# A mixer, cross-attention and routed-expert layer: 512 tokens cut as 128 + 384 in place of 256 + 256, with memory's products between the first chunk's

## The chip, the cores and the metric

One core of one Trainium2 chip runs the kernel in one launch. The time is the device time of the launch in microseconds, a median over runs. All operands lie in HBM at the start and the result is written back to HBM. The engines named below are TensorE (PE; its weight loads are PEld in the profile), VectorE (DVE), ScalarE (ACT), GpSimd (POOL), and SP, which here only issues DMAs.

## The reference

One layer over 512 tokens of width 2048, batch 1, in float32, with a memory of 256 rows. What is computed, with the parts that do not matter here left out:

```python
def reference(x, mem, ...):
    h = hybrid_mixer(x, ...)              # products with w_in (2048 x 16 K columns), mLSTM (4 heads),
                                          # forgetting attention (16 heads), both causal over the tokens,
                                          # two branch products, a gate each, w_out
    x = layer_norm(ALPHA * x + h, ...)
    h = memory_cross_attention(x, mem, w_xq, w_xkv, w_xo)    # 4 heads of 512, 256 memory rows
    x = layer_norm(ALPHA * x + h, ...)
    h = peer_ffn(x, peer_wq, sub_keys, expert_u, expert_v)
    return layer_norm(ALPHA * x + h, ...)

def peer_ffn(x, w_pq, sub_keys, expert_u, expert_v):
    q = (x @ w_pq).reshape(B, S, 8, 2, 128)
    sc = einsum('bshpd,hpnd->bshpn', q, sub_keys)            # 8 heads x 2 x 128 keys
    ...  # top 16 of each 128, top 16 of their 256 sums: 128 of 16384 experts a token, weights g
    a = einsum('tkd,td->tk', expert_u[idx], x)
    return einsum('tk,tkd->td', gelu(a) * g, expert_v[idx])
```

Each token uses 8 x 16 = 128 experts, each a row of `expert_u` and a row of `expert_v` of 8 KB. The mixer is causal: a later token needs the keys and values of earlier ones and never the other way round, so the tokens can be processed in chunks.

## The kernel before

**Products.** A weight matrix lies in HBM as groups of 2048 x 512, each four loads of 1 MB (`load_raw`, three buffers `raw`, issued on SP). Each half of a load is split by `split` into a high part and the rest (`whi`, a cast on ScalarE, L137; `wlo`, a subtraction on VectorE, L138), two buffers of each, and a product is three matmuls: high times high, high times low, low times high. `group_ws` keeps the weights stationary and streams the activations' 256 token columns (L165); `group_as` keeps the activations stationary, 128 tokens at a time, and streams 512 weight columns (L206, L207, L214). A group's sums lie in PSUM banks of a pool `mm` with five buffers; an `evac` function takes them out. Small products of the heads and transposes use three other banks (`sm_bank`).

```python
def split(hi, lo, src):
    nc.scalar.copy(hi, src)
    return nc.vector.tensor_sub(lo, src, hi.bitcast(F32))
def load_raw(src):
    raw = wp.tile([P, 2048], F32, tag="raw", bufs=3, name=nm("raw"))
    nc.sync.dma_start(raw, src)
```

**Order.** The 512 tokens are two halves of 256. The program is written in this order:

1. The gates of all 512 tokens from `xT`, which leaves every token's x split in SBUF.
2. First half: `ml_stage` (per head a group for q and k, one for v, one for o; then four pairs of gate and branch groups: 20 groups), `fx_stage` (per four heads q, k, v; then four gate and four branch groups: 20 groups), `residual` with w_out (4 groups), `norm`. Keys, values and convolution tails go to DRAM scratch or stay in `tail`, for the second half.
3. `mem_stage`: for each of 4 heads, memory's keys times w_xq and memory's values times w_xo (64 loads of 1 MB), stored to DRAM as `Ad` and `Bd` by DMAs on POOL's queue. With these, cross-attention is two products: `attend` with `Ad` (2 groups) and a `residual` with `Bd` (2 groups).
4. First half: `attend`, `residual`, `norm`.
5. Second half: the first group of `ml_stage(1)`, then `pick0`: the choice of experts (`choose`: 4 groups of `peer_wq`, `select`, `soften`) for the first half, whose indices go to `ei` and weights to `gg`. From here the gathers can run. Then the rest of the second half's mixer and its end.
6. `choose` for the second half, then the dense weights `gd`: for each token a one-hot of 128 for either key index (L1023, L1025 on VectorE), a matmul, a copy on ScalarE (L1030), a store.
7. Dense experts for the second half: `stage_a` (128 chunks of `uT`, Gelu) runs 32 chunks ahead, `stage_o` multiplies by `gd` and by `vD` and adds into `acc`.

**Gathers.** The first half's 256 tokens do not take the dense way. For each of the two blocks of 128 tokens there are 128 jobs `job_u` and 128 `job_v`. A job is one indirect DMA on POOL (L826) that fetches one row of 8 KB for each of 128 tokens, 1 MB, into one of two buffers `rows`, and one VectorE instruction that uses it: a dot product with the token (`rows`, `x2l`, L851) or an addition into `gacc` (L865).

```python
def job_v(t, k, s):
    rows = gather("peer_v", t, k, s)
    def use(s2):
        ...
        i = nc.vector.scalar_tensor_tensor(acc, rows, d[:, GB + k % GB:GB + k % GB + 1], acc,
                                           op0=ALU.mult, op1=ALU.add)
        after(i, s2)
```

Each weight split calls `tick`. It adds `rate` to a credit; each whole credit emits the next job, whose DMA may not go before that split; its use is emitted `LAG` = 2 ticks later and may not stand before that tick's split in VectorE's order. The rate is 240 jobs in 400 ticks in the second half's mixer and the rest over 490 ticks in the dense stage.

A planner (the framework's list scheduler, with a simulated timeline) then fixes each engine's order: it may take later work first where earlier work is not ready in its simulation. So a gather's use can stand far behind the tick that emitted it. After the last use of a block, `fin_early` normalizes and stores it; `fin` does the same for a dense block.

## Time and profile before

| | us |
|---|---|
| median of 3 runs | 5213.6 |
| range of the runs | 5212.26 to 5215.16 |
| profiled execution | 5213.9 |
| its span, first to last instruction | 5212.2 |
| PE busy in it | 4571.0 |
| VectorE busy | 3851.3 |
| ScalarE busy | 2051.6 |
| POOL busy | 791.8 |
| moved by DMA | 1435.57 MB, mean 275 GB/s |

The span is one execution as the hardware profiler saw it. A matmul's busy time overlaps that of the next, since matmuls are pipelined, so what one costs in a row of them is read from the distance of their starts. "Clock" in a view is the granted TensorE clock as a share of full speed, the DMA share is the mean busy share of 16 DMA engines. The profile's cut into stages used below follows the first and last loads of each matrix.

### The profile page before, as it was taken

How to read it: one execution, taken by the hardware profiler on the slowest of the kernel's cores; microseconds unless marked ns; L12 is line 12 of the kernel's file. 1: busy time of each engine (PE TensorE's matmuls, PEld its weight loads, DVE VectorE, ACT ScalarE, POOL GpSimd, SP SyncE). 2: the span in 40 equal slices, each digit the busy share in tenths (PEclk: the TensorE clock that was granted, in tenths of full speed). 3: DMA queues.
4: the chain of work that ended last, by engine and by line, in shares of the span. 5: the costliest groups of instructions: out<-in, count | busy, mean ns of one | idle time of the engine just before them, and what ended most of it. 6: DMA issues, size and time to landing. Idle time of an engine off the chain costs nothing. (4 is left out here: it accounts for less than half of the span.)

```text
span 5212.2 us, 74619 instructions
## 1 busy us (share of the span) xinstructions
PE 4571.0 (88%) x29998; PEld 4159.8 (80%) x29998; DVE 3851.3 (74%) x5446; ACT 2051.6 (39%) x2665; POOL 791.8 (15%) x676
## 2 busy tenths in 40 slices
PE   9999999999999999998999786967999999999100
PEld 8899999989989878987897586856988889998100
DVE  6654544564458997788878899998788888888655
ACT  5543444454445444444444432323444344444000
POOL 0000000000100022222222222211211112221221
PEclk9999999999999999999999898968999999999555
DMA  5555555666655588988889888977989888898777
GB/s 208 191 188 196 189 187 185 212 212 222 224 206 189 203 320 334 348 321 315 330 338 337 323 329 291 350 238 262 347 335 342 339 333 339 326 342 332 244 252 235
DMA packets 261100, 1435.57 MB, mean 275 GB/s; under 512 B 26668, under 2 KB 68972, under 8 KB 99216
## 3 DMA queue, kind: packets, MB, share of 16 engines
q1 hardware_dynamic: 135360, 831.45, 43.6%
q0 software_dynamic: 85008, 573.23, 30.2%
q10 hardware_dynamic: 40384, 26.12, 1.7%
q8 instruction: 235, 3.85, 0.3%
q14 instruction: 113, 0.93, 0.0%
HBM read 1372.59 MB, written 58.11 MB: 274 GB/s over the span
## 5 line engine op out<-in xcount | busy, mean ns | idle before, releaser
L138 DVE TENSOR_TENSOR wlo<-raw,whi 128x1024 fp32r<-128x1024 f32 x1216 | 1472.7, 1220 | 739.7 <-ACT whi L137 692.3
L137 ACT CAST whi<-raw 128x1024 fp32r<-128x1024 f32 x1216 | 1268.0, 1049 | 1719.5 <-PE mm L165 930.6
L865 DVE SCALAR_TENSOR_TENSOR gacc<-rows,dots,gacc 128x2048 f32<-128x2048 f32 x256 | 600.5, 2346 | 123.8 <-DMA rows<-in_peer_v,ei 122.8
L851 DVE SCALAR_TENSOR_TENSOR rows<-rows,x2l 128x2048 f32<-128x2048 f32 x256 | 584.9, 2285 | 106.2 <-DMA rows<-in_peer_u,ei 106.0
L826 POOL DMA_INDIRECT rows<-in_peer_v,ei x256 | 385.4, 1506 | 1268.9 <-DVE gacc L865 1085.7
L826 POOL DMA_INDIRECT rows<-in_peer_u,ei x256 | 316.5, 1236 | 1601.9 <-DVE rows L851 1065.1
L1054 PE MATMUL pa<-Ch,whi 128*128 128x256 f32 x2048 | 506.3, 284 | 34.7 <-ACT sc L815 25.7
L1055 PE MATMUL pa<-Cl,whi 128*128 128x256 f32 x2048 | 505.7, 284 | 0.0
L1054 PEld LDWEIGHTS pa<-Ch,whi 128*128 128x128 f32 x2048 | 394.3, 193 | 42.2 <-ACT sc L815 25.9
L1108 PE MATMUL mm<-vh,hph 128*128 128x512 f32 x1024 | 400.7, 393 | 19.1 <-ACT hph L137 16.6
L1109 PE MATMUL mm<-vh,hpl 128*128 128x512 f32 x1024 | 400.5, 392 | 5.8 <-DVE hpl L138 5.8
L1055 PEld LDWEIGHTS pa<-Cl,whi 128*128 128x128 f32 x2048 | 394.7, 193 | 5.0
L165 PE MATMUL mm<-Cl,whi 128*128 128x256 f32 x1536 | 379.2, 284 | 4.4 <-DVE Cl L138 4.4
L165 PE MATMUL mm<-Ch,whi 128*128 128x256 f32 x1536 | 381.2, 285 | 0.1
L165 PE MATMUL mm<-Ah,whi 128*128 128x256 f32 x1536 | 379.2, 284 | 0.3 <-ACT whi L137 0.3
L165 PE MATMUL mm<-Bh,whi 128*128 128x256 f32 x1536 | 377.8, 283 | 0.7 <-ACT whi L137 0.7
L165 PE MATMUL mm<-Al,whi 128*128 128x256 f32 x1536 | 377.5, 283 | 0.0
L165 PE MATMUL mm<-Bl,whi 128*128 128x256 f32 x1536 | 377.4, 283 | 0.0
L138 DVE TENSOR_TENSOR vl<-raw,vh 128x1024 fp32r<-128x1024 f32 x256 | 307.2, 1221 | 71.3 <-ACT vh L137 64.0
L137 ACT CAST vh<-raw 128x1024 fp32r<-128x1024 f32 x256 | 265.5, 1050 | 195.2 <-PE mm L1109 165.7
L1059 PE MATMUL pa<-Ch,wlo 128*128 128x256 f32 x2048 | 290.0, 285 | 16.8 <-DVE wlo L138 16.4
L165 PEld LDWEIGHTS mm<-Cl,whi 128*128 128x128 f32 x1536 | 295.5, 193 | 5.6 <-DVE Cl L138 4.9
(338 smaller groups left out, 8992.1 us busy)
## 6 DMA issues: line engine op xcount, KB each, us to landing
raw<-in_w_in SPq DMA_DIRECT2D x256, 1024.0 KB, 4.9
raw<-in_uT SPq DMA_DIRECT2D x128, 1024.0 KB, 6.8
raw<-in_vD SPq DMA_DIRECT2D x128, 1024.0 KB, 6.8
raw<-in_w_br_ml SPq DMA_DIRECT2D x32, 1024.0 KB, 5.2
raw<-in_w_br_fx SPq DMA_DIRECT2D x32, 1024.0 KB, 5.1
raw<-in_w_out SPq DMA_DIRECT2D x32, 1024.0 KB, 5.5
raw<-in_w_xkv SPq DMA_DIRECT2D x32, 1024.0 KB, 5.9
raw<-in_peer_wq SPq DMA_DIRECT2D x32, 1024.0 KB, 5.8
```

Source lines behind the costliest of these rows:

```text
L137: nc.scalar.copy(hi, src)
L138: return nc.vector.tensor_sub(lo, src, hi.bitcast(F32))
L165: i = nc.tensor.matmul(o, w, x, start=start, stop=stop)
L826: i = nc.gpsimd.indirect_dma_start(out=rows, out_offset=None, in_=I[table], in_offset=bass.IndirectOffsetOnAxis(ap=ei[t][:, k:k + 1], axis=0))
L851: i = nc.vector.scalar_tensor_tensor(rows, rows, 1.0, tok[t]["x2l"], op0=ALU.mult, op1=ALU.mult, accum_out=d[:, k % GB:k % GB + 1])
L865: i = nc.vector.scalar_tensor_tensor(acc, rows, d[:, GB + k % GB:GB + k % GB + 1], acc, op0=ALU.mult, op1=ALU.add)
L1054: nc.tensor.matmul(bank[:, :H], uh[:, sl], xh, start=k == 0, stop=False)
L1055: nc.tensor.matmul(bank[:, :H], uh[:, sl], xl, start=False, stop=False)
L1059: nc.tensor.matmul(bank[:, :H], ul[:, sl], X2[k][0], start=False, stop=k == 15)
L1108: nc.tensor.matmul(banks[t][g], a[:, tt], vh[:, gs_], start=c == c0, stop=False)
L1109: nc.tensor.matmul(banks[t][g], b[:, tt], vh[:, gs_], start=False, stop=False)
```

## The change

The tokens are cut into a first block of 128 and a second chunk of 384.

- **First block, mixed with memory.** `ml0` and `fx0` are the mixer for 128 tokens; every group is a `group_as` with one block. All groups are now generators that stop after each 1 MB load. `mix(first_block(), ms, MIX)` takes three steps of the first block's mixer and w_out, then one of `mem_stage`. While this runs there is a second pair of raw buffers (`wx`); alone, `wp` has two, no longer three.
- **First block's end.** `Ends(…, 0, 1, …)` does attention, residual and norm for 128 tokens, then `pick0` chooses for that block, after the chunk's first group as before. The 256 jobs of block 0 are spread over 1040 units; a split counts 3 units in a group over 384 tokens, 2 over 256, 1 over 128.
- **Second chunk.** `ml1` and `fx1` run 384 tokens; `group_ws` streams 384 columns into four banks of one PSUM buffer each, `group_as` does three blocks. The x of these tokens is loaded and split a second time.
- **Split at w_out.** From w_out on the chunk is block 1 (`e1`, 128 tokens, gathered later) and blocks 2 and 3 (`e2`, 256 tokens, dense). Their steps alternate, block 1 ahead; block 1's choice (`pick1`) then stands before the last norm of blocks 2 and 3.
- **Gathers.** Block 1's 256 jobs are added after `pick1`, over 1070 units of the choice and the dense stage (a `uT` split counts 2.1, a `vD` split 2). The lag is 2, then 3 from the dense weights on. The credit is capped at 2.
- **One-hots.** Four tokens at once: two broadcast comparisons of 128 x 512 on VectorE, then four scalings by `g` on ScalarE (in place of 4 + 4 instructions on VectorE, whose second did the scaling).
- **Dense stage.** Two more raw buffers in the pool `main`, used in turn with `wp`'s two. A gathered block's final affine rows are now 1 MB each, in the `rows` buffers, loaded for the gathered block and again for the dense blocks.

The core of the diff:

```diff
-LAG = 2
-EARLY = 240
+MIX = 3
...
+        def mix(a, b, n):
+            live = True
+            for i, _ in enumerate(a):
+                if live and i % n == n - 1:
+                    live = next(b, 0) is None
...
-            raw = wp.tile([P, 2048], F32, tag="raw", bufs=3, name=nm("raw"))
-            nc.sync.dma_start(raw, src)
+            raws["n"] += 1
+            p = raws["pools"][raws["n"] % len(raws["pools"])]
+            raw = p.tile([P, 2048], F32, tag="raw", bufs=2, name=nm("raw"))
+            nc.sync.dma_start(raw[:, :n], src)
...
-        def group_ws(src, X, evac):
+        def group_ws(src, X, nb, evac):
+            n = nb * P
+            per = 2 if nb == 2 else 1
-            banks = [mm_bank() for _ in range(2)]
+            banks = [mm_bank() for _ in range(4 // per)]
...
-            state["credit"] += state["rate"]
+            state["credit"] = min(state["credit"] + state["rate"] * cost, 2.0)
...
-                state["later"].append((n + LAG, f(t, k, s)))
+                state["later"].append((n + state["lag"], f(t, k, s)))
+        def set_rate(units):
+            state["rate"] = (len(jobs) - state["done"]) / units
...
+        raws["pools"].append(wx.enter_context(pool("wx", side="right")))
+        def first_block():
+            with pool("ml0") as mp:
+                yield from ml0(mp, hT, m0)
+            with pool("fx0") as fp:
+                yield from fx0(fp, yT, m0, G0)
+            e["x"] = Ends(e["xs"].enter_context(pool("xa0")), 0, 1, nc.gpsimd, nc.gpsimd)
+            yield from e["x"].residual(G0, I["w_out"], True, 4)
...
+                mix(first_block(), ms, MIX)
+                e["x"].norm(0, X1, pr0, False)
+                drain(ms)
+        wx.close()
...
+        drain(e["x"].attend(X1, pr0, PT))
+        drain(e["x"].residual(PT, Bv, False))
+        e["x"].norm(1, X2, pr0, True)
+        def pick0():
+                c = Choice(pp, pp, 1)
+                drain(c.run(X2, nc.gpsimd))
+                c.indices(0)
+            add_jobs(0)
+            set_rate(1040.0)
+            ticks.append(tick)
+            drain(ml1(mp, X, prB, hT, pick0))
+        drain(fx1(X, prB, yT, prA, G))
...
+        drain(e1.residual(Gb, I["w_out"], True))
+        e1.norm(0, X1b, pr1, False)
+        drain(e2.residual(Gc, I["w_out"], True))
+        drain(e1.attend(X1b, pr1, PTb))
+        e2.norm(0, X1c, lambda: pair(cpl, "X", 16), False)
+        drain(e1.residual(PTb, Bv, False))
+        drain(e2.attend(X1c, pr1, PTc))
+        e1.norm(1, X2b, pr1, True)
+        drain(e2.residual(PTc, Bv, False))
+            drain(c.run(X2b, nc.sync))
+            c.indices(1)
+        add_jobs(1)
+        set_rate(1070.0)
+        e2.norm(1, X2, lambda: pair(fpl, "X", 16), True)
+            drain(c.run(X2, nc.sync))
+        state["lag"] = 3
...
-                        nc.vector.tensor_scalar(o1, iota, selT["i1"][:, c], None, op0=ALU.is_equal)
-                        nc.vector.tensor_scalar(o0, iota, selT["i0"][:, c], selT["g"][:, c],
-                                                op0=ALU.is_equal, op1=ALU.mult)
+                    nc.vector.tensor_tensor(o1, selT["i1"][:, ta:ta + 4].unsqueeze(2).to_broadcast(full), it,
+                                            op=ALU.is_equal)
+                    nc.vector.tensor_tensor(o0, selT["i0"][:, ta:ta + 4].unsqueeze(2).to_broadcast(full), it,
+                                            op=ALU.is_equal)
+                        nc.scalar.activation(o0[:, u], o0[:, u], AF.Copy, scale=selT["g"][:, ta + u:ta + u + 1])
...
+        raws["pools"].append(mn)
-        state["rate"] = (len(jobs) - state["done"]) / 490.0
```

More of the change, by code (lines that the diff above doesn't have):

```diff
@@ L321, in mt, with ml1 @@
+        def ml1(mp, X, hpool, hT, between):
+            n = 384
             def mt(tag, bufs, n=512):
@@ L359, in ev_o @@
                     nc.scalar.activation(ot[t], b, AF.Sigmoid)
[L361 to L362 removed]
+                yield from group_ws(wi[3 * h], X, 3, ev_qk)
+                if h == 0:
                     between()
[L364 to L371 removed]
@@ new lines, in build, with __init__, t, residual @@
+        class Ends:
+            def __init__(self, xp, b0, nb, ld, st):
+                self.xp, self.b0, self.nb, self.ld, self.st = xp, b0, nb, ld, st
+                self.r = [[None] * 4 for _ in range(nb)]
+            def t(self, tag, bufs, n=512):
+                return self.xp.tile([P, n], F32, tag=tag, bufs=bufs, name=nm(tag))
+            def residual(self, X_, W, first, rbufs=12):
+                nb, r = self.nb, self.r
+                self.sts = self.xp.tile([P, 2, 32], F32, tag="sts", bufs=3, name=nm("rst"))
@@ L901, in build, with tick @@
                     jobs.append((job_v, t, k - lag))
-        order = []
-        for i in range(HB):
-            order += [(j, i) for j in jobs if j[1] == i]
-        jobs = [j for j, _ in order]
-        def tick(s):
+        def tick(s, cost):
             n = state["n"] = state["n"] + 1
@@ new lines, in build @@
+        e = {}
+        with pool("memt", side="right") as tp:
+            MT = []
+            for i in range(2):
+                raw = load_raw(I["memT"][i])
+                for q in range(4):
+                    a, b = pair(tp, "M", 16)
+                    split(a, b, raw[:, q * 512:(q + 1) * 512])
+                    MT += parts(a, b, MEM)
+            with pool("mem", side="right") as xp:
+                ms = mem_stage(xp, MT)
+                mix(first_block(), ms, MIX)
+                X1, X2 = [], []
+                e["x"].norm(0, X1, pr0, False)
+                drain(ms)
@@ new lines, in build, with prA @@
+        wx.close()
+        del raws["pools"][1:]
+        big = ExitStack()
+        ap_ = big.enter_context(pool("bigA", side="right"))
+        def prA():
+            return pair(ap_, "A", 32, 384)
+        X = []
+        for i in range(4):
+            raw = load_raw(I["x1T"][i], 1536)
+            for q in range(4):
+                a, b = prA()
+                split(a, b, raw[:, q * 384:(q + 1) * 384])
+                X.append((a, b))
+        PT = []
+        drain(e["x"].attend(X1, pr0, PT))
@@ L1117, in stage_o @@
             if last and dh == 0:
+                if state["done"] < len(jobs):
+                    raise RuntimeError(f"{len(jobs) - state['done']} jobs left")
+            if last and dh:
+                while state["later"]:
+                    state["later"].pop(0)[1](s)
                 fin_load()
```

1074 lines of the change are left out of this document (574 added, 500 removed).

## The prediction

> **What bounds the kernel now.** I read the page's slices first, then the stretches between stage borders, then the DMA issues of four of them, the waits, and the chain at the end.
>
> ```profile
> span 5212.2 us, 74619 instructions
> PE   9999999999999999998999786967999999999100
> PEclk9999999999999999999999898968999999999555
> DMA  5555555666655588988889888977989888898777
> ```
>
> TensorE is full for 37 of 40 slices and then idle: the last three hold no matmul, while DMA goes on. The DMA row has two levels: five or six tenths in the first 15 slices, nine from the 16th on, when the row gathers begin.
>
> ```profile
> 20.00:972.00 952.00, 951.20 (x6772) 891.91 (x6770) 516.11 (x775) 438.54 (x552) 36.64 (x68) 1.00 0.54 190
> 972.00:1067.00 95.00, 95.00 (x484) 81.41 (x483) 53.53 (x55) 38.91 (x39) 3.22 (x6) 1.00 0.62 215
> 1067.00:1447.00 380.00, 368.91 (x2716) 348.67 (x2715) 197.35 (x209) 171.58 (x206) 35.72 (x56) 1.00 0.65 219
> 1447.00:1600.00 153.00, 152.51 (x863) 133.28 (x862) 94.83 (x121) 80.22 (x107) 9.13 (x17) 1.00 0.59 206
> 1600.00:1800.00 200.00, 199.60 (x1302) 180.60 (x1302) 194.45 (x618) 93.66 (x110) 3.09 (x2) 1.00 0.52 181
> 1800.00:2735.00 935.00, 888.23 (x6193) 820.46 (x6192) 755.42 (x898) 396.90 (x497) 207.81 (x142) 0.98 0.88 329
> 2735.00:3035.00 300.00, 254.06 (x1272) 210.69 (x1271) 258.39 (x277) 131.47 (x172) 72.23 (x50) 0.91 0.89 327
> 3035.00:3570.00 535.00, 404.33 (x2780) 365.35 (x2779) 510.69 (x1233) 162.98 (x279) 91.75 (x78) 0.87 0.81 285
> 3570.00:4835.00 1265.00, 1240.64 (x7551) 1113.28 (x7552) 1038.18 (x1075) 520.03 (x675) 249.73 (x159) 0.99 0.89 337
> 4835.00:5212.00 377.00, 8.02 (x35) 5.99 (x33) 221.25 (x174) 6.48 (x12) 77.33 (x81) 0.52 0.72 246
> ```
>
> Columns: stretch, length, then busy us and count of PE, PEld, DVE, ACT, POOL, then clock, DMA share, GB/s. In order: first half's mixer, its w_out, memory's products, first half's cross-attention, its choice of experts with the second half's first group; second half's mixer, its end, second choice with the one-hot build, dense experts, tail. PE bounds the mixers, memory and the dense stage; DVE bounds both choices (194 of 200, 511 of 535); the tail is bounded by gathers.
>
> Gathers issued in 1780 to 2735, 3035 to 3570, 3570 to 4835, 4835 to 5212 (count, size or none, median us to landing), with one weight load beside the first and the uncontended one:
>
> ```profile
> rows<-in_peer_u,ei POOLq DMA_INDIRECT x78, 8.1
> rows<-in_peer_v,ei POOLq DMA_INDIRECT x66, 8.2
> raw<-in_w_in SPq DMA_DIRECT2D x106, 1024.0 KB, 7.0
> ...
> rows<-in_peer_u,ei POOLq DMA_INDIRECT x39, 6.5
> rows<-in_peer_v,ei POOLq DMA_INDIRECT x39, 7.6
> ...
> rows<-in_peer_u,ei POOLq DMA_INDIRECT x80, 7.7
> rows<-in_peer_v,ei POOLq DMA_INDIRECT x79, 8.2
> ...
> rows<-in_peer_v,ei POOLq DMA_INDIRECT x47, 5.5
> rows<-in_peer_u,ei POOLq DMA_INDIRECT x34, 5.5
> ...
> raw<-in_w_xqT SPq DMA_DIRECT2D x16, 1024.0 KB, 4.8
> ```
>
> So 144 of the 512 gathers go out in the second mixer (6.6 us each), 50 in its end (the POOL count above), 78, then 159 beside the dense stage (8.0 us each), and 81 are left when the matmuls end. These cost 377 us: 342 of gathering (4.2 us each) and 35 of finish. The chain of the end is made of such landings, two at a time, each with its use on DVE:
>
> ```profile
> 4863.86 5.46 DMA rows<-in_peer_v,ei
> ```
>
> Waits in the dense stage (total us, times, longest):
>
> ```profile
> POOL rows L826 <- DVE rows L851: 492.9, 64, 14.4
> POOL rows L826 <- DVE gacc L865: 437.1, 70, 13.0
> ...
> DVE gacc L865 <- DMA rows<-in_peer_v,ei: 8.8, 5, 2.8
> ```
>
> POOL waits 930 us for a row buffer; DVE hardly waits for rows. With two row buffers, a landing of 8 us and a place in DVE's fixed order, 8 us a gather is what this stage gives.
>
> **Prices.** Start to start, a 256-column matmul takes 0.12 us, a 512-column one 0.225:
>
> ```profile
> 100.77 0.28 PE L165 MATMUL mm<-Ah,whi 128*128 128x256 f32 x1
> 100.89 0.28 PE L165 MATMUL mm<-Al,whi 128*128 128x256 f32 x1
> ...
> 4822.05 0.39 PE L1108 MATMUL mm<-vh,hph 128*128 128x512 f32 x1
> 4822.28 0.39 PE L1109 MATMUL mm<-vh,hpl 128*128 128x512 f32 x1
> ```
>
> A group (2048x512 weights, four 1 MB loads, 8 splits) is 192 matmuls with weights stationary (23.0 us at 256 columns) or 48 per 128 tokens with tokens stationary (10.8). The first mixer bears it out: 28 groups x 23.0 + 12 x 21.6 = 904, so 48 of its 952 us are heads. For 384 columns no row exists. Bounds: 0.12 and 0.225; I take the middle by length, 0.173, so 33.2 us a group (23 to 43). The Trainium skill, "TensorE: Matmul & The Clock Gate", back-to-back issue gap, has N/2.4 + 2.5 ns: an estimate of 162.5 ns at 384, by which the sum would fall by 27 x 192 x 0.0105 = 54 us; its 216 ns at 512 stands against 225 here.
>
> ```profile
> L138 DVE TENSOR_TENSOR wlo<-raw,whi 128x1024 fp32r<-128x1024 f32 x1216 | 1472.7, 1220 | 739.7 <-ACT whi L137 692.3 <-PE mm L165 27.2 <-PE mm L214 17.5
> L137 ACT CAST whi<-raw 128x1024 fp32r<-128x1024 f32 x1216 | 1268.0, 1049 | 1719.5 <-PE mm L165 930.6 <-PE mm L207 456.8 <-DVE wlo L138 154.6
> L865 DVE SCALAR_TENSOR_TENSOR gacc<-rows,dots,gacc 128x2048 f32<-128x2048 f32 x256 | 600.5, 2346 | 123.8 <-DMA rows<-in_peer_v,ei 122.8 <-ACT stage L1030 0.7
> L1025 DVE TENSOR_SCALAR o<-iota,i0T,gT 128x128 f32<-128x128 f32 x256 | 85.1, 334 | 0.0
> L1023 DVE TENSOR_SCALAR o<-iota,i1T 128x128 f32<-128x128 f32 x256 | 70.3, 276 | 0.2 <-PE mm L1027 0.2
> L770 DVE TENSOR_TENSOR eq<-pf,iota 128x512 f32<-128x512 f32 x32 | 20.3, 675 | 0.0
> L506 ACT COPY pt<-sm 128x128 f32<-128x128 f32 x32 | 8.7, 271 | 0.0
> ```
>
> **The change, part by part.**
>
> *A, first block mixed with memory.* 44 groups of 128 tokens (40 mixer, 4 w_out): 44 x 10.8 = 475. Memory is unchanged, 363 of its 380 us by count (48 loads x 5.76 + 16 x 5.4). Heads about 45 (half of 48 and the added transposes). PE: 883. Against it: 240 MB plus some 22 MB of stores, operands and x; at the 337 GB/s of the dense stage 810 us. DVE: 480 splits x 1.22 = 586, plus half of the first mixer's other work (516 - 390 = 126, so 63) and memory's (41): 690. All fit, none with much room: a 128-token half-load has 1.36 us of PE against a 1.22 us subtraction, on two whi/wlo buffers. I add 40 for that and 20 of start: A ends at 945. Ends: 905 with perfect cover, 1060 if each of the 352 half-loads waited 0.5 us. The block's small loads and memory's 64 stores share POOL's queue: 37 + 36 us of its busy time, with no gather behind them. The other 384 tokens' x is split twice, for the gates here and again in B: 32 splits of 128x384, under 1.22 us each, 39 at most, beside PE's first groups.
>
> *B, first block's end, and its choice.* Attention 2 groups, residual 2, choice 4, chunk two's first group 33. Raw buffers are now two: 0.4 + 4.8 landing + about 3.4 for both splits, over two, is 4.3 us a load against 2.7 of PE, so 32 loads cost 138; with norm 15, the last selection 25 and half of the first group hidden: 205, to 1150 (150 to 270). Gathers begin there, not at 1800.
>
> *C, chunk two, 384 tokens.* 27 x 33.2 + 12 x 32.5 = 1286; heads 1.5 x 53 = 80. Four of five PSUM banks go to a weights-stationary group, so the next one waits for evacuation: some 20 such borders x 1.5 us = 30 (0 if ScalarE empties them in time, 80 if four 0.6 us copies are waited out each time and DVE's are behind a 2.3 us gather step). C: 1396, ends 2546. SP's queue holds kp, vp, nF and m1 behind the raw loads; a raw load now waits for one of two buffers, with 16.6 us of PE per pair against 7.0 + 3.4, so I cost that at nothing; that cover goes if landings pass 9 us. The 256 gathers of block one are due over 1040 units of the 936 here and 224 behind (5.6 us each); at the 6.6 measured they end at 2840, still ahead of the next choice.
>
> *D, ends of blocks two (128) and three to four (256), and block two's choice.* 48 thin loads x 4.4 + 32 x 5.5 = 387, the norms of one beside the products of the other, 30 for the last selection: 418, to 2964. The old end was 300 for 32 loads with its norms bare. Ends: 340 and 530 (7.0 us landings all along).
>
> *E, second choice and build.* DVE decides: selection for two blocks about 130 (194 of the first choice less its 40 splits and a group's convolution), splits 39 + 78 (32 uT chunks ahead), last norm 25, the one-hots 128 x 0.675 = 86 in place of 155, and gathers. The ticks allow only 47 here (choice 64 and chunks 134 units at 256/1070), x 2.35 = 110. Sum 468, at 96% 485. The 256 added scalings on ScalarE, x 0.27 = 69, lie in its idle time (163 of 535 busy); they show only if it is late for a bank. To 3449.
>
> *F, dense stage.* Same matmuls: 1265, to 4714. Lag 3 and four raw buffers I cost at nothing: the gathers run behind their due time, so the lag does not bind, and PE is not waiting for loads (1241 of 1265). Gathers at 8.0 us: 159. Left: 256 - 47 - 159 = 50.
>
> *G, tail.* 50 x 4.1 = 205, finish 40 (35, with the affine rows loaded twice). End: 945 + 205 + 1396 + 418 + 485 + 1265 + 245 = 4959, say 4960. This is a sum of spans; the profiled execution took 1.7 us more than its span (5213.9) and lies 0.3 above the median of three, so nothing is corrected. Differences under 0.2% (10 us) I call the same.
>
> **Rivals.**
>
> *R1, gathers keep up.* For it: only 256 are left after block two's choice, where 318 were left at 3035, and DMA in D is free. Against: 159 in the dense stage was with POOL always holding due jobs. If the stage gave 195 (6.5 us, the second mixer's rate), 14 would be left: 4714 + 57 + 40 = 4811.
>
> *R2, thin loads starve.* Steps of 2.7 us of PE wait for two raw buffers and a busy DVE; A takes 1060, D 530, so the second gathers start 227 later and the end is 5187, a gain of half a percent only. For it: the end stage at 300 us for 173 of PE now. The granted clock falls where PE waits, 0.91 in 2735 to 3035 and 0.52 in the tail; at 0.5 a thin load has 5.4 us of PE in place of 2.7, 1.0 above the 4.4 counted in D, so 48 us more there, within D's upper end. The Trainium skill, "TensorE: Matmul & The Clock Gate", HAM oscillation, says the same of thin products: waits beyond 3.4 us put PE back on half clock at every step; the two clocks agree in kind.
>
> *R3, slower: PSUM banks in C.* If each of the 39 groups stalled PE for evacuation behind DVE's gather steps, at 8 us a group C grows by 312 - 30 = 282 and the end is 5241. It passes the old time at 7.3 us a group. Against: ScalarE, which empties most banks, was 42% busy there (397 of 935), and PE's longest total wait in the old second mixer (1800 to 2735) was for a softmax, 18 us over ten heads:
>
> ```profile
> PE sm L501 <- DVE p L492: 18.2, 10, 3.0
> ```
>
>
> *R4, the tail does not move.* The fixed order defers block two's gathers to the end as before (81 or more left), with stages as forecast: 4714 + 332 + 40 = 5086.
>
> **How the numbers follow.** Forecast 0.47 (4870 to 5040), R1 0.20, R4 0.15, R2 0.09, R3 0.09. A range 4790 to 5180 takes in R1, R4 and most of the forecast's spread, and leaves R3 and the ends of others, about 2 in 10. Faster 0.87 (forecast, R1, R4, most of R2), same 0.03, slower 0.10.
>
> **What would show it.** A: w_out's last load of block one near 930, DMA share about 0.85 there. B: first gather near 1150. C: about 1400 us, 384-column starts 0.17 apart. D: the second 256 gathers start near 2960. E: dense stage starts near 3450 with DVE above 0.95. F: 155 to 165 gathers beside 1265 us. G: 50 gathers behind the last matmul. The prediction is wrong if the first weights of the dense stage come later than 3600, or if the count left at the last matmul is under 20 or over 80.

## The result, and the profile after

The changed kernel takes 5249.5 us (median of 4 runs, 5243.4 to 5252.4) against 5212.9 of the kernel before (4 runs, 5209.8 to 5215.2): a ratio of 1.0069 [1.0052, 1.0086]. It is slower by 0.7 per cent; 4960 had been forecast. The profiled span grew from 5212.2 to 5241.7 us.

The page of the kernel before, its row of TensorE's total, and then the page of the changed kernel: the span, the totals, and three rows of slices.

```profile
PE 4571.0 (88%) x29998; PEld 4159.8 (80%) x29998; DVE 3851.3 (74%) x5446; ACT 2051.6 (39%) x2665; POOL 791.8 (15%) x676
```

```profile
span 5241.7 us, 66469 instructions
PE 4565.4 (87%) x25662; PEld 4021.7 (77%) x25662; DVE 3915.7 (75%) x5122; ACT 2272.1 (43%) x3129; POOL 811.7 (15%) x631
PE   7999999789999999999978887369999999999700
DMA  7888888557777887776878657159998888888767
```

TensorE has the same work as before, 4565 against 4571 us: fewer and wider matmuls, no less time. It is no longer full in the first slice and around the eighth, it has a hole at slices 21 to 27 where the old one had a smaller hole, and it is still idle in the last two. The stretches of the changed kernel, in the order of the prediction's letters A to G (columns as in the prediction: stretch, length, busy us and count of PE, PEld, DVE, ACT, POOL, clock, DMA share, GB/s; POOL's count from C on is gathers). The fourth and fifth rows are cut at 3040, ahead of block two's query weights; the forecast's D runs on to block two's indices, which come at 3177:

```profile
20.00:940.00 920.00, 888.98 (x5040) 758.54 (x5039) 677.99 (x757) 618.83 (x727) 55.00 (x90) 0.99 0.82 303
940.00:1150.00 210.00, 161.83 (x688) 122.27 (x687) 146.94 (x286) 109.63 (x150) 6.44 (x12) 0.92 0.61 216
1150.00:2650.00 1500.00, 1462.29 (x7637) 1327.50 (x7636) 1083.45 (x1419) 514.07 (x695) 334.81 (x228) 0.99 0.75 278
2650.00:3040.00 390.00, 325.22 (x1324) 249.84 (x1323) 295.07 (x341) 185.13 (x240) 47.69 (x28) 0.90 0.74 271
3040.00:3510.00 470.00, 295.78 (x1793) 261.58 (x1791) 371.90 (x1000) 224.24 (x520) 19.04 (x17) 0.83 0.49 167
3510.00:4945.00 1435.00, 1414.99 (x9093) 1288.76 (x9094) 1155.69 (x1166) 606.10 (x775) 278.30 (x177) 1.00 0.88 332
4945.00:5242.00 297.00, 7.68 (x28) 5.83 (x27) 176.29 (x141) 5.86 (x11) 65.28 (x63) 0.52 0.71 247
```

Put against the forecast, with a third column that the first experiment below supplies (the run-ahead put back):

| stage | forecast | changed kernel | with run-ahead |
|---|---|---|---|
| A, to its end | 945 | 940 | 940 |
| B | 205 | 210 | 210 |
| C | 1396 | 1500 | 1500 |
| D, to block two's indices | 418 | 527 | 525 |
| E | 485 | 333 | 470 |
| F | 1265 | 1435 | 1265 |
| G | 245 | 297 | 255 |
| sum | 4959 | 5242 | 5165 |

**Where the time came from, against the kernel before.** As TensorE's work is the same, the end of the matmuls can only move by its idle time. Stretch minus busy, from the rows here, in the prediction and in experiment 1 (the ends and the second choice cut at 3035 and 3040):

| idle TensorE, us | before | changed | with run-ahead |
|---|---|---|---|
| first tokens, memory, first choice | 13 | 79 | 78 |
| the second mixer | 47 | 38 | 37 |
| its ends | 46 | 65 | 66 |
| second choice and build | 131 | 174 | 144 |
| dense stage | 24 | 20 | 14 |
| sum | 261 | 376 | 339 |

So TensorE is idle for 115 us more, and the matmuls end 110 us later (4945 in place of 4835). The tail is 80 shorter (297 in place of 377), because 63 gathers are left in place of 81. 110 - 80 = 30, which is the 29.5 us of the spans. The earlier gathers did bring something; the added idle time took more: 66 us in the first three stages, 19 in the ends and 43 in the second choice and build, of which the blocked queue described next made 30 (elsewhere it is 13 less).

**The hole at slice 26.** SP issues all weight loads through one queue. First the waits of that queue, from 3200 to 3530, with the columns: waiting line, waited for, total us, times, longest:

```profile
SPq L154 <- DMA gd<-stage: 151.8, 3, 128.1
```

then its issues from 3196 on in the changed kernel:

```profile
3196.86 36.92 SPq L154 DMA_DIRECT2D raw<-in_peer_wq  x6
3240.18 156.28 SPq L154 DMA_DIRECT2D raw<-in_uT  x5
3500.37 1.54 SPq L1275 DMA_DIRECT2D G<-gd  x2
```

and in the kernel before:

```profile
3100.76 213.43 SPq L142 DMA_DIRECT2D raw<-in_uT  x25
3317.72 0.33 SPq L835 DMA_DIRECT2D x2l<-x2d  x1
3320.07 37.08 SPq L142 DMA_DIRECT2D raw<-in_uT  x7
```

The old kernel loads 32 chunks of `uT` ahead beside the choice and the build. In the changed one every second load goes to a raw buffer of pool `main`, whose memory still holds the `stage` tiles of the one-hot build; the load waits for their stores, and all loads behind it wait too, in order. DMA stands nearly still:

```profile
3250.00:3380.00 130.00, 38.86 (x217) 35.30 (x216) 119.61 (x428) 35.90 (x110) 3.02 (x3) 0.65 0.12 44
```

Six loads of `uT` go out before 3510, and the run-ahead's products (32 chunks) are done in F instead, which is why F has 1415 us of TensorE in place of 1241.

**The second gathers.** The gathers of the changed kernel around the border of its two blocks (start, us, instruction, idle before it and what ended it):

```profile
2886.59 0.94 POOL L983 DMA_INDIRECT rows<-in_peer_v,ei  x1 [9.86 <-DVE wlo L148]
3177.65 0.94 POOL L983 DMA_INDIRECT rows<-in_peer_u,ei  x1 [290.12 <-DVE ei L969]
```

For 290 us no gather runs: block one is done, and block two's indices `ei` come only at 3177, forecast for 2964.

### The profile page after: what moved, and what is told of

Its sections match the earlier page's. It is cut to its first block, busy times and chain, and to the rows that moved or that the text cites. A ratio compares the mean times of both kernels' runs of the same rounds, so it can differ in the third digit from the quotient of the medians.

```text
span 5241.7 us, 66469 instructions
## 1 busy us (share of the span) xinstructions
PE 4565.4 (87%) x25662; PEld 4021.7 (77%) x25662; DVE 3915.7 (75%) x5122; ACT 2272.1 (43%) x3129; POOL 811.7 (15%) x631
## 5 line engine op out<-in xcount | busy, mean ns | idle before, releaser
L1259 PE MATMUL pa<-Xh,whi 128*128 128x256 f32 x2048 | 503.9, 283 | 32.0 <-ACT whi L147 21.1
L1260 PE MATMUL pa<-Xl,whi 128*128 128x256 f32 x2048 | 503.2, 283 | 0.0
L179 PE MATMUL mm<-Ah,whi 128*128 128x384 f32 x1280 | 439.6, 344 | 8.2 <-DVE qk L612 3.0
L179 PE MATMUL mm<-Al,whi 128*128 128x384 f32 x1280 | 435.6, 341 | 0.0
L1259 PEld LDWEIGHTS pa<-Xh,whi 128*128 128x128 f32 x2048 | 389.9, 190 | 39.4 <-ACT whi L147 21.5
L1260 PEld LDWEIGHTS pa<-Xl,whi 128*128 128x128 f32 x2048 | 388.8, 190 | 6.5
L223 PE MATMUL mm<-whi,Zh 128*128 128x512 f32 x832 | 333.9, 401 | 48.1 <-ACT whi L147 45.9
L224 PE MATMUL mm<-whi,Zl 128*128 128x512 f32 x832 | 331.2, 398 | 1.1 <-DVE Zl L148 1.1
L223 PE MATMUL mm<-whi,Ah 128*128 128x512 f32 x768 | 314.2, 410 | 7.5 <-ACT whi L147 7.5
L224 PE MATMUL mm<-whi,Al 128*128 128x512 f32 x768 | 311.8, 406 | 0.0
```

The lines of the kernel that those rows point to most:

```text
L179: i = nc.tensor.matmul(o, w, x, start=start and s % per == 0, stop=stop and s % per == per - 1)
L223: nc.tensor.matmul(banks[t], xh[:, tt], wh[:, c], start=k == 0, stop=False)
L224: nc.tensor.matmul(banks[t], xl[:, tt], wh[:, c], start=False, stop=False)
L1259: nc.tensor.matmul(bank[:, :H], uh[:, sl], xh, start=k == 0, stop=False)
L1260: nc.tensor.matmul(bank[:, :H], uh[:, sl], xl, start=False, stop=False)
```

## The experiments

All ratios are to the kernel before, in runs on the same chip. The kernel before took 5208.7 to 5217.6 us (medians) beside the different experiments, so a difference of some 10 us between two experiments says little.

**1. The run-ahead put back.** Pool `main` gives its raw buffers only behind the chunks that run ahead.

```diff
         mn = ctx.enter_context(pool("main"))
-        raws["pools"].append(mn)
...
         for a in range(ahead[0]):
             stage_a(a)
+        raws["pools"].append(mn)
```

> Changed kernel with one line moved: the two raw buffers of pool main join only after the 32 uT chunks ahead are written, so that these use the two buffers of wp alone. Theory P (the new raw buffers lie on memory that the one-hot build still uses, so SP's queue stands at them and holds the run-ahead and its gathers): over 30 uT loads and over 40 gathers go out between block two's choice and the start of the dense stage (6 and 17 in the changed kernel), the dense stage takes about 1265 in place of 1435, the last matmul comes near 4800 in place of 4945, 30 to 45 gathers are left (63), the time is 5040 to 5120. Theory G (the gathers decide, two row buffers at 8 us each from block two's choice on, wherever PE is): the loads go ahead too, but what PE gains comes back as more gathers left, 80 to 95, time 5190 to 5250.

5160.8 us (5155.0 to 5166.9), 0.9902 [0.9886, 0.9919]. Its stretches from 3040 on:

```profile
3040.00:3645.00 605.00, 460.89 (x3218) 421.88 (x3216) 507.71 (x1104) 298.73 (x615) 58.31 (x47) 0.92 0.65 230
3645.00:4910.00 1265.00, 1251.02 (x7677) 1125.06 (x7678) 1036.72 (x1073) 532.89 (x681) 222.22 (x155) 0.99 0.89 335
4910.00:5165.00 255.00, 0.84 (x4) 0.38 (x2) 153.47 (x126) 3.76 (x8) 54.56 (x54) 0.51 0.70 254
```

The blocked queue cost 89 us, and without it the change is a gain of 1 per cent. Theory P has the mechanism and not the size: the last matmul comes at 4910, not near 4800, and 54 gathers are left. F is 1265 as forecast, with 155 gathers. The stretch from 3040 to the dense stage, called the choice stretch below, is 605 us with the run-ahead in it; 470 of them lie behind block two's indices (3175), where the forecast's E had 485.

**2. Memory behind the first block, not mixed with it.**

```diff
-                mix(first_block(), ms, MIX)
+                mix(first_block(), ms, 10 ** 6)
```

> Changed kernel, with memory's products after the first block and not between its steps. Theory M (the first block alone would be bound by DMA, 12.4 us a group at 340 GB/s against 10.8 of PE, with four raw buffers): 44 groups 545 and memory 380, so the stretch to the first block's end is 945 to 970 in place of 940, time +5 to +40. Theory S (a thin load's two splits and two products follow each other through two whi/wlo buffers, about 2 us a half load): 44 groups 700 and memory 380, time +130 to +160. If mixing costs anything: time below 5240.

5268.7 us (5266.2 to 5276.6), 1.0118 [1.0101, 1.0135], 19 us slower than the changed kernel, inside theory M's range. The mixing is worth no more than that: 79 us of idle TensorE stay with it up to the first choice.

**3. The old one-hots.** Each one-hot made whole on DVE as before, in place of batches of four that ScalarE scales.

```diff
-                    nc.vector.tensor_tensor(o1, selT["i1"][:, ta:ta + 4].unsqueeze(2)..., it, op=ALU.is_equal)
-                    nc.vector.tensor_tensor(o0, selT["i0"][:, ta:ta + 4].unsqueeze(2)..., it, op=ALU.is_equal)
...
-                        nc.scalar.activation(o0[:, u], o0[:, u], AF.Copy, scale=selT["g"][:, ta + u:ta + u + 1])
+                        nc.vector.tensor_scalar(o1, iota, selT["i1"][:, c], None, op0=ALU.is_equal)
+                        nc.vector.tensor_scalar(o0, iota, selT["i0"][:, c], selT["g"][:, c],
+                                                op0=ALU.is_equal, op1=ALU.mult)
```

> Changed kernel with the one-hots of before, two VectorE instructions of 128x128 a token and no scaling on ScalarE. If VectorE sets the length of that stretch, which has 155 us of it in place of 86: build 40 to 70 us longer, time +40 to +70. If the stretch in the changed kernel is set by ScalarE's scalings instead (PE waited 43 us for them): build within 20 us, time within 15 of the changed kernel.

5223.7 us (5220.7 to 5238.7), 1.0033 [1.0019, 1.0048]: 26 us faster than with the batches, a miss for every theory stated. The batches do save DVE work, but the build has waits in turns: from 3200 to 3530 of the changed kernel DVE waited for PE 59.5 us, PE for ScalarE's scaled `o` 42.6 us:

```profile
DVE o L1226 <- PE mm L1233: 59.5, 42, 7.2
PE mm L1233 <- ACT o L1232: 42.6, 29, 6.6
```

**4. Lag 2 in place of 3.**

```diff
-        state["lag"] = 3
```

> Changed kernel with the lag left at 2 in the dense stage. As predicted (gathers run behind their due time there, so the lag does not bind): 175 to 180 gathers beside the dense stage, time within 10 us. Rival (a lag of 3 holds the uses back and so the row buffers): 185 to 195 gathers there, 45 to 55 left, time -30 to -80.

5239.5 us (5225.5 to 5245.9), 1.0061 [1.0044, 1.0078], 63 gathers left as in the changed kernel: the lag does not bind, as forecast.

**5. Run-ahead and old one-hots together.** Edits 1 and 3.

> The run-ahead mended as in e1 and, beside it, the one-hots of before. Theory K (the batched one-hots cost by their chain, comparison, scaling on ScalarE, matmul, through two buffers each: VectorE waited 58 us for matmuls there and PE 39 for scalings): the stretch from block two's choice to the dense stage is 20 to 60 us shorter than e1's 605, time 5100 to 5145. Theory V (VectorE's busy time sets that stretch, 508 of 605 in e1, and the old one-hots add 69): stretch 40 to 70 longer, time 5190 to 5230.

5167.7 us (5154.5 to 5176.2), 0.9923 [0.99, 0.9946], no different from edit 1 alone, and neither theory's time; the choice stretch is 597. The 26 us of experiment 3 are gone once chunks run ahead beside the build.

**6. Run-ahead, and rings of four for the batched one-hots.** Edit 1, and `bufs=4` for `o1` and `o0`.

> e1 with four in place of two buffers for the batched one-hots o1 and o0. Theory K2 (of that chain the two buffers are what holds): VectorE's wait for those matmuls falls from 58 to under 20 us, the stretch of 605 loses 25 to 60, time 5105 to 5140. Theory A (ScalarE's four scalings, two copies and casts in a row set the pace of the build, whatever the buffers): wait of PE for scalings stays near 39, time within 12 of e1's 5161.

5164.2 us (5155.8 to 5175.5), 0.9923 [0.9907, 0.994]; the choice stretch is 590. PE's wait for ScalarE's `o` fell from 38.9 to 21.8 us, and DVE's for PE from 58.0 to 41.4, without effect on the time, which is theory A's.

**7. A third row buffer in the dense stage**, in place of main's raw buffers.

```diff
+            gat["n"] = gat.get("n", 0) + 1
+            if "more" in gat and gat["n"] % 3 == 0:
+                return gat["more"].tile([P, D], F32, tag="rows", bufs=1, name=nm(n))
...
-        raws["pools"].append(mn)
...
+        gat["more"] = mn
```

> e1 without the extra raw buffers of pool main (two raw buffers in the dense stage) and with a third row buffer for the gathers from the dense stage on. Theory B2 (two row buffers and a landing of 8 us set 8 us a gather there): 185 to 215 gathers beside the dense stage in place of 155, under 20 left, PE as before, time 5010 to 5070. Theory D (DMA at 0.89 is full, the weights take their share first): 155 to 170 gathers, landings of 10 us and more, time 5130 to 5170. Mixed case: more gathers, but PE waits for two raw buffers and the dense stage takes 1300 to 1350.

5107.5 us (5101.0 to 5112.4), 0.9803 [0.9786, 0.9819]. Its dense stage:

```profile
3650.00:5100.00 1450.00, 1298.86 (x7632) 1131.15 (x7632) 1177.01 (x1180) 528.10 (x684) 427.31 (x208) 0.98 0.87 334
```

All 208 gathers run beside it, 7.0 us each in place of 8.2 in experiment 1, and the tail is gone; but TensorE is idle 151 us there in place of 14, mostly waiting for split weights. This is the mixed case, at a higher price than it named (1300 to 1350): 255 us of tail were exchanged for a last matmul 190 us later. The run also has two raw buffers fewer there, so this loss is not the row buffer's alone.

**8. Block two's choice ahead.** On top of experiment 5, the norm and choice of block two stand ahead of the cross-attention heads and second residual of blocks three and four, and its gathers are spread over 1134 units.

```diff
         drain(e1.residual(PTb, Bv, False))
-        drain(e2.attend(X1c, pr1, PTc))
...
         e1.norm(1, X2b, pr1, True)
-        drain(e2.residual(PTc, Bv, False))
...
-        set_rate(1070.0)
+        set_rate(1134.0)
+        drain(e2.attend(X1c, pr1, PTc))
...
+        drain(e2.residual(PTc, Bv, False))
```

> e8 with block two's norm and choice moved ahead of blocks three and four's attention and second residual; its jobs over 1134 units. Theory T (the gathers of block two start too late: from 2861 to 3070 none run while DMA is at 0.6 to 0.7): their start comes 80 to 120 us earlier, 15 to 25 more are out at the start of the dense stage, 25 to 40 left, time 5030 to 5080 or 50 to 90 below e8. Rival N (the norms and block two's selection are then bare, with nothing beside them): the ends take 40 to 80 us longer and the time is within 20 of e8's.

5130.3 us (5119.0 to 5137.3), 0.9845 [0.9826, 0.9864]; the first of the second gathers starts here:

```profile
3101.61 0.94 POOL L983 DMA_INDIRECT rows<-in_peer_u,ei  x1 [211.61 <-DVE ei L969]
```

Against experiment 5 the gathers start 71 us earlier (3102 in place of 3172), 43 are left in place of 54, and the time is 37 us shorter, between the two theories. These 71 us of the indices' delay were worth that much.

**9. Both: third row buffer and choice first.** Edits 7 and 8, with the batched one-hots.

> No main raw buffers; every third gather goes to a third row buffer that is made behind the run-ahead of the dense stage (as in the run with that buffer alone, 5107 us), and the second block's norm and choice stand ahead of the other mixer's heads and residual (as in the run that had the choice first, whose gathers began 73 us earlier). If the gathers' start and the buffers are two separate debts, the effects add: with the third buffer the gathers were already all done beside the dense stage, so the earlier start only thins them; what is won is the PE's lost time, up to 1450 - 1262 = 188 us of the dense stage for the part of the gathers that moves ahead of it: 20 to 70 us, 5040 to 5090. Rival: the dense stage with three buffers is bounded by DVE and DMA work that does not change with the start: 5095 to 5115.

5117.1 us (5105.6 to 5122.0), 0.9801 [0.9783, 0.9819]: the gains do not add. 196 gathers run beside a dense stage of 1439 us and no tail is left, so that an earlier start has nothing more to shorten. The time is 2 us above the rival's range.

**10. The third row buffer in the kernel before.**

```diff
+            gat["n"] = gat.get("n", 0) + 1
+            if "more" in gat and gat["n"] % 3 == 0:
+                rows = gat["more"].tile([P, D], F32, tag="rows", bufs=1, name=nm("rows"))
+            else:
-            rows = gat["pool"].tile([P, D], F32, tag="rows", bufs=gat["rows"], name=nm("rows"))
+                rows = gat["pool"].tile([P, D], F32, tag="rows", bufs=gat["rows"], name=nm("rows"))
...
             stage_a(a)
+        gat["more"] = mn
```

> The kernel before with one edit: every third gather of the dense stage goes to a third row buffer, made behind its run-ahead. If it is the two row buffers that set how many gathers run beside the dense stage, the old kernel's 81 gathers left over drop to under 25 and the gain is what the run with the third buffer showed on the changed kernel, some 2 per cent: 5090 to 5150. Rival: the buffers bind only with the new order of the first stage: 5190 to 5220.

5010.5 us (5004.7 to 5021.4), 0.9600 [0.9584, 0.9616], the fastest kernel of this study and better than either theory expected. Its page's slices, and its stretches from the second choice on:

```profile
PE   9999999999999999999899977695799999999992
DMA  5555555566665478998888988797799999999996
```

```profile
3035.00:3580.00 545.00, 411.23 (x2823) 374.33 (x2821) 513.78 (x1235) 166.24 (x283) 91.47 (x79) 0.86 0.78 281
3580.00:4921.00 1341.00, 1263.01 (x7580) 1122.11 (x7581) 1184.16 (x1180) 519.51 (x680) 358.34 (x225) 0.99 0.95 370
4921.00:5020.00 99.00, 1.25 (x6) 0.71 (x4) 66.64 (x70) 1.99 (x5) 24.90 (x16) 0.52 0.67 239
```

Three row buffers give a gather each 6.0 us (225 in 1341) where two gave 8.0 (159 in 1265); the stage is 76 us longer, the tail 278 shorter. One more buffer, against the bound that the prediction named for the dense stage, was worth more than all that the change moves.

**11. No gap between the blocks.** Edit 1, and block two's gathers follow block one's at once, on block one's indices.

```diff
             add_jobs(0)
-            set_rate(1040.0)
+            add_jobs(1)
+            set_rate(2230.0)
...
-                                             in_offset=bass.IndirectOffsetOnAxis(ap=ei[t][:, k:k + 1], axis=0))
+                                             in_offset=bass.IndirectOffsetOnAxis(ap=ei[0][:, k:k + 1], axis=0))
```

> The run-ahead is kept (main raw buffers made behind it). Block two's gathers follow block one's at once: they use block one's indices, weights and second rows, so block two's own choice is left out of what they compute, though it is still worked out beside them. If the gap of 290 us between the two blocks' gathers is what the forecast missed (with the queue's block already undone), then with gathers at 4.4 to 6 us each some 50 to 65 more are done before the dense stage; under 10 are left for the end, the tail is 60 to 90 us in place of 258, and the time is 4960 to 5010. Rival: the gathers moved into the gap slow the stage between the blocks by about what they save, and the time is 5080 to 5170.

5148.0 us (5144.0 to 5152.2), 0.9869 [0.9853, 0.9886], 13 us faster than experiment 1. Its stretches from C to the dense stage:

```profile
1150.00:2650.00 1500.00, 1472.95 (x7726) 1341.58 (x7727) 1080.19 (x1423) 522.89 (x705) 312.30 (x216) 0.99 0.73 272
2650.00:3040.00 390.00, 323.44 (x1297) 244.58 (x1295) 313.59 (x351) 181.97 (x234) 61.02 (x42) 0.92 0.81 303
3040.00:3635.00 595.00, 457.28 (x3158) 420.61 (x3158) 516.48 (x1108) 290.27 (x602) 74.56 (x54) 0.90 0.65 238
```

312 gathers are done by the dense stage in place of 303: 21 more in the last two rows, 12 fewer in C, as 512 gathers are now paced over 2230 units (0.23 a unit) in place of 256 over 1040 (0.25). The run closed the gap and thinned the gathers ahead of it, so it shows that the gap by itself is cheap at this pace; it doesn't show what a gap closed at the old pace in C would bring. The time lies in the rival's range, but not for its reason: the stage between the blocks wasn't slowed, and few gathers were won.

**12. Experiment 9 with a fifth raw buffer in the dense stage**, and gathers due over 900 units.

```diff
-            p = raws["pools"][raws["n"] % len(raws["pools"])]
-            raw = p.tile([P, 2048], F32, tag="raw", bufs=2, name=nm("raw"))
+            one = "one" in raws and raws["n"] % 3 == 0
+            p = raws["one"] if one else raws["pools"][raws["n"] % len(raws["pools"])]
+            raw = p.tile([P, 2048], F32, tag="raw", bufs=1 if one else 2, name=nm("raw"))
...
-        set_rate(1134.0)
+        set_rate(900.0)
...
         gat["more"] = mn
+        raws["one"] = mn
```

> The kernel with the third row buffer and the choice first, and besides a fifth raw buffer made behind the run-ahead and gathers due each 900 in place of 1134 units. If the loads of the dense stage wait for raw buffers when three gathers are in flight (PE waited 55.6 us in all for the split weights there), the fifth buffer gives back part of that: 5000 to 5070. Rival: the DMA's share of 0.87 is what the two kinds of transfer have between them, and the time stays within 10 us of the run without it.

(The expectation calls it the fifth; as main has no other raw buffers in this kernel, it is the third beside two.) 5069.7 us (5062.0 to 5072.2), 0.9712 [0.9696, 0.9728]: the dense stage falls from 1439 to 1350 us. The choice stretch ahead of it grows from 670 to 710, with 74 gathers in it in place of 60, so the last matmul comes 49 us earlier. Which of the two edits brought this is not shown. This is the best that the new order reached.

**13. Half of the one-hots scaled on ScalarE, half made on DVE.** On top of experiment 6.

```diff
-                    nc.vector.tensor_tensor(o0, selT["i0"][:, ta:ta + 4]..., op=ALU.is_equal)
+                    nc.vector.tensor_tensor(o0[:, 0:2], selT["i0"][:, ta:ta + 2]..., op=ALU.is_equal)
...
+                        if u < 2:
                             nc.scalar.activation(o0[:, u], o0[:, u], AF.Copy, scale=selT["g"][:, c])
+                        else:
+                            nc.vector.tensor_scalar(o0[:, u], iota, selT["i0"][:, c], selT["g"][:, c], ...)
```

> The kernel with the run-ahead and rings of four for the one-hots (5164 us), and of each four one-hots two are scaled on ScalarE and two made whole on DVE. In the one-hot build (3500 to 3645 of the run-ahead kernel) ScalarE was busy 105 of 145 us, DVE 78. If the build is a chain through ScalarE, with DVE's idle time unused, moving half the scalings takes 40 us from ScalarE and the build shrinks to some 115 us: E 560 to 575 and 5130 to 5145 in all. Rival: the build's pace is that of PE and its banks, and E stays at 590 to 605, 5155 to 5170.

5153.6 us (5151.7 to 5157.6), 0.9875 [0.9857, 0.9894], between the two theories' ranges. The build's stretch of experiment 1 and of this one:

```profile
3500.00:3645.00 145.00, 84.92 (x500) 77.59 (x498) 77.62 (x121) 105.45 (x353) 1.14 (x1) 0.85 0.43 124
```

```profile
3500.00:3635.00 135.00, 83.66 (x568) 79.32 (x567) 94.47 (x237) 76.44 (x242) 7.04 (x3) 0.82 0.54 164
```

ScalarE lost 29 us of work and the build lost 10 of length; no engine is full in either. Experiment 6, whose buffers this run shares, already had a choice stretch of 590 us with every scaling on ScalarE; here it is 595. So ScalarE's work is not what sets its length.

**14. Four raw buffers beside the thin products and the run-ahead.**

```diff
         cpl = cs.enter_context(pool("x1c", side="right"))
+        raws["pools"].append(cpl)
...
         cs.close()
+        del raws["pools"][1:]
...
         bb.close()
+        raws["pools"].append(ctx.enter_context(pool("rw")))
...
-        raws["pools"].append(mn)
```

> The changed kernel with its two extra raw buffers in other places: beside cross-attention's thin products, then from the second choice on (behind the blocks' ends) to the end, and none in pool main. No queue is blocked, and the run-ahead has four raw buffers in place of two. If two buffers starve the thin products and the run-ahead, the ends of blocks two to four drop from 390 by 20 to 40 us and the second choice from 605 by 30 to 60: 5070 to 5115. Rival: DVE and the order of the work set these stages, and the time is that of the kernel with the run-ahead and two buffers, 5150 to 5170.

5176.5 us (5158.8 to 5185.8), 0.9916 [0.9886, 0.9946]: no different from experiment 1. The first part of the choice stretch, with four raw buffers and with two (experiment 1):

```profile
3040.00:3500.00 460.00, 378.20 (x2739) 348.46 (x2738) 429.78 (x983) 191.97 (x252) 63.88 (x47) 0.93 0.73 269
```

```profile
3040.00:3500.00 460.00, 375.96 (x2720) 344.29 (x2719) 430.08 (x984) 193.28 (x262) 57.17 (x46) 0.95 0.71 264
```

DVE is busy 430 of 460 us in both. More raw buffers change nothing, as the rival had it, and its reason, DVE and the order of its work, fits these rows; the time is 6 us above its range.

**15. Experiment 10 with earlier due times.**

```diff
-EARLY = 240
+EARLY = 264
...
-        state["rate"] = (len(jobs) - state["done"]) / 490.0
+        state["rate"] = (len(jobs) - state["done"]) / 470.0
```

> The kernel before with the third row buffer (5010 us), and its first gathers paced for 264 in place of 240 in each 400 steps, those of the dense stage over 470 in place of 490 steps. The run without that had 16 gathers behind the last matmul and 99 us of tail. If the schedule's pace and not a resource left these, the tail drops to the 35 to 45 us of the finish: 4950 to 4980. Rival: the dense stage's DMA, busy 0.95 of the time, gives no more, and the time stays within 10 us of 5010.

5023.2 us (5010.6 to 5028.4), 0.9624 [0.9599, 0.9648], 13 us above experiment 10, with overlapping intervals: near the rival's value. The tail shrank, as the first theory had it, but the last matmul moved from 4921 to 4994: it looks as if what the gathers take earlier, the weights get later. DMA is at 0.95 from 3580 to 4940 there.

**16. Four raw buffers early and the third row buffer, in the new order.** Edit 14 and the third row of experiment 7, with `GA` 23 in place of 26.

> The kernel with the four raw buffers early, and besides every third gather of the dense stage goes to a third row buffer in pool main; three fewer buffers for spilled gates pay for its memory. If raw buffers and row buffers were all that the new order lacked, the tail goes (40 us) and the dense stage is 1300 to 1340, as the old order's was with three row buffers: 4960 to 5020. Rival: the new order's idle TensorE in the thin stages stays, and with 20 to 30 us more gathers in the dense stage the time is 5040 to 5090.

5077.3 us (5076.4 to 5085.6), 0.9735 [0.9715, 0.9755], the rival's value, and 67 us above experiment 10.

**The two orders with row buffers out of the way.** Experiment 12 against 10, by the idle time of their stretches: the first tokens with memory and the first choice 80 against 13 us, the second mixer 40 against 49, its ends 78 against 44, second choice and build 167 against 134, dense stage 80 against 78, in sum 444 against 317. These 127 us less the 79 of tail that the new order saves (20 against 99) are 48 of the 51 us between the spans (5070.4 and 5019.7).

## Why the prediction was wrong

**The sum was not held against TensorE's total.** No product is removed by the change, and the page had 4571.0 us of them. Matmuls that end at 4714, as forecast, leave some 140 us for all idle time up to there, where the kernel before had 261. The forecast's own A alone had 62 (945 less 883), and its B and D were stages of waits. The terms that were too small are these.

**C, 104 us too long: the heads.** The step "heads 1.5 x 53 = 80" took the old 935 us stretch to hold 39 groups. It held fewer; this is the stretch's product rows in the kernel before:

```profile
L165 PE MATMUL mm<-Ch,whi 128*128 128x256 f32 x1152 | 284.6, 284 | 0.0
L165 PE MATMUL mm<-Bh,whi 128*128 128x256 f32 x464 | 113.9, 283 | 0.0
L206 PE MATMUL mm<-whi,Ch 128*128 128x512 f32 x269 | 106.6, 396 | 0.0
```

64 such matmuls make a weights-stationary group and 32 a tokens-stationary one: 25.25 and 8.4 groups, 582 + 182 = 764 us. Most of the other five groups lay ahead of the stretch. So heads and waits were 171 us there, 124 of them TensorE's. In the changed kernel C holds 26.7 x 33.2 + 12 x 32.5 = 1276 of products, and 186 of heads (1462 less 1276), which is 1.5 x 124. So heads are 106 us more than the 80 counted, idle time is 38 in place of 30, and products are 10 less than 1286. The pace of 384 columns was right:

```profile
1748.05 0.34 PE L179 MATMUL mm<-Ah,whi 128*128 128x384 f32 x1
1748.22 0.34 PE L179 MATMUL mm<-Al,whi 128*128 128x384 f32 x1
```

Starts lie 0.173 us apart, the middle that was chosen between 256 and 512 columns. The estimate of 162.5 ns from the Trainium skill, "TensorE: Matmul & The Clock Gate", back-to-back issue gap, lies below it; the measurement decides.

**D, 109 us too long: the thin loads and the last selection.** The forecast had block two's indices at 2964; they came at 3177, so D is 527 us in place of 418. It counted 387 us for 80 loads. From 2650 to the copy of block two's last query, at 3128, these took 478, or 6.0 us each in place of 4.8. The last selection then took 49 us in place of 30, beside the norm and the first splits for blocks three and four; DVE was busy 76.6 of the 78 us from 3100 to 3178. The loads mostly waited for a split to give back a raw buffer, here from 2880 to 3178:

```profile
SPq L154 <- DVE wlo L148: 174.6, 34, 18.0
```

This is what R2 described, at its time of 530. Four raw buffers in the cross-attention part left 2650 to 3040 at 390 us and the indices at 3175 (experiment 14), so the buffers alone are not the cause there; how the 91 us divide between splits, norms and products stays open. With block two's choice put first, the indices came 71 us earlier and 37 us were won (experiment 8).

**E: run-ahead beside the choice.** "Lag 3 and four raw buffers I cost at nothing" was right for the lag (experiment 4) and wrong for the buffers: their memory was not free yet, and the queue stood (89 us, experiment 1). With the run-ahead in place E is 470 us for 485, and that is partly luck: DVE had 387 us of work there, not 468, and was busy 82 per cent of the time, not 96. Of its 83 idle us 67 lie in the last 145, the build. Old, deeper and mixed one-hots and more raw buffers moved the choice stretch by 15 us at most. That none of these alone sets the build is shown; what does is open.

**F and G** follow: with the run-ahead F is 1265 as forecast, 155 gathers in place of 159, and 54 are left in place of 50. In the changed kernel F also holds the blocked run-ahead, 63 gathers are left and G is 297. With the run-ahead put back the sum is 206 us above the forecast, and C and D make 211 of them.

**Right:** A (940 for 945) and B (210 for 205), the lag, the pace in the dense stage (8.1 us a gather), and its cause, two row buffers (6.0 us with three, experiment 10).

**The rivals.** R1 did not come, and R4 not quite (63 left, between 50 and 81). R2 came in D and not in A (940, not 1060). R3's time, 5241, is the measured span by luck alone: C grew by 104 us and not by 282, TensorE's longest wait there was for a split, and its waits for an evacuation come to some 6 us in all.

```profile
PE mm L179 <- DVE wlo L148: 13.9, 12, 2.5
```

**The signs.** Two of the signs named ahead showed the miss: C at 1500 for 1400, and the second gathers at 3177 for 2960. The two named for a wrong prediction did not: the count left (63) stayed inside its bounds, and the dense stage's first products started at 3283 and then starved. A late start of its second product (3693, forecast at 3449) would have been a better one.

**Readings to set right.** The old TensorE row is not full for 37 slices: six of the slices 19 to 28 read 6 to 8 tenths, and the 38th reads one. Its DMA row rises from the 15th slice, to mostly eight and nine tenths. In the first choice TensorE was busy 199.6 of 200 us beside DVE's 194, so that DVE bounds it is not shown.

## What to carry to other kernels

When a change only rearranges work, add the forecast's busy time of the bounding engine over all stages and hold it against its total on the page; what is missing there is missing in a stage. A buffer given by a new pool may be memory of an earlier stage, and a queue that issues in order then stands for everything behind it: look where a pool's memory comes from before costing it at nothing. Count the groups in a stretch by its matmul rows before dividing its time among them. And try the bound that the profile names (here a third row buffer, four per cent) before reordering around it.

## What the runs showed of the hardware

With three row buffers and three raw buffers the dense stage of the kernel before moved 370 GB/s over 1341 us with DMA busy 0.95, where two row buffers moved 337 at 0.89. The Trainium skill, "Trainium Architecture — The Big Picture", "What this means for kernel authors", gives about 360 GB/s of HBM bandwidth to a core; the trace lies 3 per cent above it. Experiment 15 had gathers done earlier at the same DMA share, and its last matmul came 73 us later; that gathers and weight loads stand in each other's way at this level fits this, and no run shows it apart.
